# A two-layer diffusion backbone: when the first two gate slabs are split, and where the head norms are turned

## The chip, the cores and the metric

The kernel runs on one core of one Trainium2 chip, on five engines with a queue of their own each: TensorE (PE, its weight loads PEld), VectorE (DVE), ScalarE (ACT), GpSimd (POOL) and SyncE (SP), which issues the DMAs. The metric is the device time of one execution in microseconds (us), the median of a few runs.

## The reference, cut to what matters

Two layers over 512 latent and 256 context tokens, 1024 wide, in float32. The second layer needs of the context only keys and values. In each layer:

```
p = modulate(rmsnorm(x)) @ w_in           # columns: conv a | conv g | q | k | v | merge gates
z = p.a * sigmoid(p.g)                    # 512 channels
conv = silu(layernorm(depthwise31(z)))    # 31 taps along the tokens
per head of 8:
    w = softmax(q1 @ k1) - lam * softmax(q2 @ k2)
    o = rmsnorm(w @ v) * (1 - lam_init)   # a factor for each head and token
g = sigmoid(p.gates + b_gate)             # 2048 columns: g_conv | g_attn
x = x + gx1 * ((g_conv * (conv @ w_conv_out) + g_attn * (o @ w_attn_out)) @ w_out)
x = x + gx2 * (relu(modulate(rmsnorm(x)) @ w_mlp1) ** 2 @ w_mlp2)
```

## The kernel before

**Three products for one.** Each float32 matrix is split into a high part, rounded for TensorE's fast float32 format, and the low part that is left; a product is three matmuls, high by high, low by high and high by low (lines 109 to 111, and `mm3`). `split` (L75 to L77) makes them: ScalarE copies the high part (L76), VectorE subtracts (L77), or GpSimd where a call says so. A weight slab of 256 columns is loaded by one DMA (`load_slab`) and split in two halves, so two high parts of 128x1024 and two low parts. Names: `r_wg` is a raw gate slab, `h_wg` its high and `l_wg` its low part, and a slab is called (1,0) for the first of the attention half of the gates, (1,1) for the second, up to (0,3). `state["behind"]` holds instructions behind which `load_slab` queues the split on their engine (`tc.issue_after`).

**The attention stage.** Heads go one by one, `attend(h)`: scores S (L722, L724), maximum, exponentials e on ScalarE (L729), their difference on VectorE (L739), transposes wT (L752) with a split into wth and wtl, the values av (`values`, L109 to L111 with vh and vl), a square osq and a copy uo on ScalarE (L767, L769), and `finish`: two sums on TensorE (L777), rsall on ScalarE (L781) and a power on GpSimd (L784). Between these steps `merge` puts other matmuls as filler, by a ratio of costs written in the code (`rc`). With the last head, number 7, the filler is the conv branch: `conv_a`, then `conv_g` with blocks cg of 128x512 (in layer 0 also 128x256 for the context), each followed by a sigmoid sg on ScalarE (L510, which needs another activation table than the exponential: ACT_TABLE_LOAD) and the multiply z on VectorE (L512). `conv_g1_ahead` loads gate slab (1,0) behind the first block of the second half, with GpSimd as the engine of its low part, and slab (1,1) at the filler's end.

**Between attention and gates.** `spill_rstd` turns the 32 (layer 0: 48) norm factors of all heads on TensorE (rsT, L814), VectorE copies them out of PSUM (rst, L816), and SP writes them to DRAM (rs_d, L817). They come back spread over the partitions (arb, L984) and are multiplied into the head outputs ar (L986), whose low parts h1l feed the attention projection ya.

**The gates.** A loop over eight slabs, the attention half first: two gate tiles gt of 24 matmuls in each for the latent tokens, one sigmoid each (L1009). The 31 taps of the convolution for each of four channel groups (`taps`, L955 and L959, accumulator cacc) are spread over VectorE's time here, `per_gate` of them behind each gate tile. Then ya, LayerNorm and the convolution's projection yc.

**What sets the order.** The order of instructions on each engine is that in which the scheduler lets them issue: each waits its turn behind what was put on its engine before, and `issue_after` adds an edge. PSUM tiles come from pools: gt, cg and rsT share two tiles of one pool (`mm_tile`).

Of the kernel before, what the change touches and what calls it, by code (L numbers as in the profile page):

```python
# [10 lines left out]
AF = mybir.ActivationFunctionType  # L11
# [40 lines left out]
def trunk_kernel(  # L52
# [6 lines left out]
    nc = tc.nc  # L59
# [389 lines left out]
    for i in range(DEPTH):  # L449
# [50 lines left out]
        def conv_g(s):  # L500
            w = conv_w.pop(("g", s), None) or conv_load("g", s)
            for m in range(2):
                cc = 2 * s + m
                for g in groups:
# [4 lines left out]
                    sgt = ap.tile([P, 768], F32, tag="e0", name=f"sg{i}_{cc}_{g.start}", bufs=2)  # L509
                    nc.scalar.activation(out=sgt[:, :W], in_=ps[:, :W], func=AF.Sigmoid)  # L510
                    zz = zt[cc][:, z0 : z0 + W]
# [4 lines left out]

        wg = {}

        def gate_slab(half, s, lo_eng=None):
            wg[half, s] = load_slab(rows(wi, G_OFF + half * D + 256 * s, 256),  # L520
                                    f"wg{i}_{half}_{s}", lo_eng=lo_eng)

        def conv_g1_ahead():

            g = conv_g(1)
            yield next(g)
            gate_slab(1, 0, nc.gpsimd)
            yield from g
            gate_slab(1, 1)

# [162 lines left out]
        def attend(h):  # L693
# [5 lines left out]
            def scores(t):  # L699
# [15 lines left out]
                for m in range(2):  # L715
                    S = pS.tile([P, 768], F32, tag="S", name=f"S{nm}_{m}")
                    for lo, hi in ((0, 512), (512, 768)):
                        lo = max(lo, kb * P)
                        if hi <= lo:
# [8 lines left out]
                    e = ap.tile([P, 768], F32, tag=f"e{m}", name=f"e{m}{nm}", bufs=2 - m)  # L728
                    nc.scalar.activation(out=e[:, :nkey], in_=S[:, :nkey], func=AF.Exp,  # L729
                                         bias=st[:, m : m + 1],  # L730
                                         accum_out=st[:, 2 + m : 3 + m])
                    es.append(e)
# [24 lines left out]
            def values(u):  # L757
# [10 lines left out]
                uo = ap.tile([P, 256], F32, tag="uo", name=f"uo{i}_{h}_{u}")  # L768
                nc.scalar.activation(out=uo, in_=av[:, :256], func=AF.Copy, scale=L["ag"])  # L769
                nc.sync.dma_start(at_d[i][h, :, 256 * u : 256 * u + 256], uo)  # L770
# [127 lines left out]
        for h in range(H):  # L898
# [14 lines left out]
            if h == H - 1:  # L913
                rest = chain_(conv_a(0), conv_a(1), conv_g(0), conv_g1_ahead())
                rc = 24.0 if last else 38.0
            fill.append(with_late(rest))
# [4 lines left out]
            merge(main, chain_(*fill), fc / att_cost)  # L921
        drain(spill_rstd())
        for pl in (psx, pspool, apool):
# [68 lines left out]
        for half, lst in ((1, ga), (0, gc)):  # L992
            for s in range(4):
                if (half, s) not in wg:
                    gate_slab(half, s)
                if half == 0 and s == 3:
                    for hg in branch[:4]:
                        branch_load(*hg)
# [389 lines left out]
```

## Time and profile before

| | us |
|---|---|
| median of three runs | 2351.58 |
| lowest and highest | 2349.04 and 2352.13 |
| the profiled execution, its own time | 2353.61 |
| its span | 2351.8 |
| TensorE busy | 2276.6 |
| VectorE busy | 1476.0 |
| ScalarE busy | 995.2 |
| GpSimd busy | 687.3 |

The span is the time from the first to the last instruction that the profile shows; the execution's own time holds 1.8 us around it. The head that ends the attention stage of layer 0 stands at about 450 to 485 us of the span, that of layer 1 at about 1740 to 1780. A granted clock of 1.00 is TensorE's upper level of 2.4 GHz; matmuls of 128x512 that take 0.63 us where others take 0.39 ran at the lower, 1.2 GHz.

### The profile page before, as it was taken

What the parts mean: (1) busy time and instruction counts of PE and PEld (TensorE: products, weight loads), DVE (VectorE), ACT (ScalarE), POOL (GpSimd) and SP (SyncE); (2) the same over time, 40 slices, a digit from 0 to 9 for tenths busy, and PEclk for the clock granted to TensorE, in tenths of its full rate; (3) what the DMA queues carried; (4) which work ended last, traced back from release to release, by engine and by line L of the source; (5) the groups of instructions that cost most, each with busy time, mean ns of one, the idle gap of its engine ahead of it and who ended that gap; (6) DMA issues with size and microseconds to landing.
All of it is one profiled execution on the core that took longest, in us unless ns stands there. A gap on an engine that the chain in (4) does not pass through costs nothing.

```text
span 2351.8 us, 36393 instructions
## 1 busy us (share of the span) xinstructions
PE 2276.6 (97%) x14626; PEld 2042.8 (87%) x14626; DVE 1476.0 (63%) x2587; ACT 995.2 (42%) x1965; POOL 687.3 (29%) x790
## 2 busy tenths in 40 slices
PE   7999999999999999999999999999899999999999
PEld 6999998888888988888888988999877879888887
DVE  6777776699656455565655465767759966433332
ACT  5556654522332362332415255655542334432432
POOL 1866764100000133232223266757610000000000
PEclk9999999999999999999999999999999999999999
DMA  9111111143535124333343211111114323223222
GB/s 313 57 42 34 44 46 44 46 160 125 180 119 175 51 81 127 115 128 115 113 130 127 89 46 57 44 43 44 61 59 141 112 90 126 90 90 98 99 90 72
DMA packets 222570, 224.76 MB, mean 96 GB/s; under 512 B 6256, under 2 KB 212544, under 8 KB 222272
## 3 DMA queue, kind: packets, MB, share of 16 engines
q1 hardware_dynamic: 222400, 222.43, 29.4%
q8 instruction: 115, 1.88, 0.3%
q14 instruction: 55, 0.45, 0.1%
HBM read 208.73 MB, written 13.67 MB: 95 GB/s over the span
## 4 chain that ended last, share of the span: by engine, by line
PE 83%; DVE 7%; ACT 4%; POOL 2%; DMA 2%; issue 1%; SPq 0%; ACTq 0%; POOLq 0%; DVEq 0%
PE r L109 6%; PE r L110 6%; PE r L111 6%; PE f L110 6%; PE f L109 6%; PE f L111 6%; PE gt L109 3%; PE gt L110 3%; PE gt L111 3%; PE qk L109 2%; PE qk L110 2%; PE qk L111 2%; PE v L109 2%; PE v L110 2%; PE v L111 2%; PE o L109 2%
## 5 line engine op out<-in xcount | busy, mean ns | idle before, releaser
L110 PE MATMUL f<-h2l,h_w 128*128 128x512 f32 (+1 forms) x832 | 284.5, 343 | 1.1 <-POOL h2l L77 1.1
L109 PE MATMUL f<-h2h,h_w 128*128 128x512 f32 (+1 forms) x832 | 282.9, 343 | 2.2 <-ACT h2h L76 1.7
L111 PE MATMUL f<-h2h,l_w 128*128 128x512 f32 (+1 forms) x832 | 283.0, 342 | 0.0
L109 PE MATMUL r<-fh,h_w 128*128 128x512 f32 (+1 forms) x832 | 283.0, 341 | 0.0
L110 PE MATMUL r<-fl,h_w 128*128 128x512 f32 (+1 forms) x832 | 282.9, 340 | 0.0
L111 PE MATMUL r<-fh,l_w 128*128 128x512 f32 (+1 forms) x832 | 282.8, 340 | 0.0
L77 POOL TENSOR_TENSOR l_w<-r_w,h_w 128x1024 fp32r<-128x1024 f32 x64 | 157.8, 2487 | 339.5 <-ACT h_w L76 339.5
L76 ACT ACTIVATE h_w<-r_w 128x1024 fp32r<-128x1024 f32 x128 | 128.6, 1052 | 254.3 <-PE r L110 117.2
L959 DVE SCALAR_TENSOR_TENSOR cacc<-z,cols,cacc 128x783 f32<-128x783 f32 (+1 forms) x240 | 201.2, 891 | 0.3
L279 DVE SCALAR_TENSOR_TENSOR adaac<-ar,cvec,adaac 128x256 f32<-128x256 f32 x336 | 160.8, 541 | 44.6 <-DMA ar<-in_w_ada_dram 22.7
L109 PE MATMUL qk<-h_wqk,h1h 128*128 128x256 f32 x640 | 183.3, 289 | 0.7 <-ACT h1h L76 0.7
L1154 DVE SCALAR_TENSOR_TENSOR X<-r,ad,X 128x512 f32<-128x512 f32 (+1 forms) x104 | 65.1, 625 | 189.0 <-PE r L111 188.8
L110 PE MATMUL qk<-l_wqk,h1h 128*128 128x256 f32 x640 | 180.6, 284 | 0.0
L111 PE MATMUL qk<-h_wqk,h1l 128*128 128x256 f32 x640 | 176.9, 285 | 0.3 <-POOL h1l L77 0.3
L726 DVE TENSOR_REDUCE st<-S 128x1 f32<-128x768 f32 (+1 forms) x160 | 134.7, 846 | 66.8 <-PE S L724 65.3
L109 PEld LDWEIGHTS f<-h2h,h_w 128*128 128x128 f32 x832 | 158.1, 191 | 21.1 <-ACT h2h L76 2.3
L110 PEld LDWEIGHTS f<-h2l,h_w 128*128 128x128 f32 x832 | 159.1, 191 | 19.6 <-POOL h2l L77 1.9
L111 PEld LDWEIGHTS f<-h2h,l_w 128*128 128x128 f32 x832 | 158.8, 191 | 17.7
L111 PEld LDWEIGHTS r<-fh,l_w 128*128 128x128 f32 x832 | 157.7, 190 | 17.7
L109 PEld LDWEIGHTS r<-fh,h_w 128*128 128x128 f32 x832 | 157.7, 190 | 17.4
L110 PEld LDWEIGHTS r<-fl,h_w 128*128 128x128 f32 x832 | 157.8, 190 | 17.2
L1235 DVE TENSOR_TENSOR fl<-fr,fh 128x512 fp32r<-128x512 f32 (+1 forms) x104 | 67.9, 659 | 138.4 <-ACT fr L1234 138.2
(255 smaller groups left out, 6297.7 us busy)
## 6 DMA issues: line engine op xcount, KB each, us to landing
r_w<-in_w_mlp_dram SPq DMA_DIRECT2D x64, 1024.0 KB, 5.4
ada<-in_w_ada_dram SPq DMA_DIRECT2D x24, 1024.0 KB, 6.1
ar<-in_w_ada_dram SPq DMA_DIRECT2D x48, 512.0 KB, 3.5
r_wqk<-in_w_in_dram SPq DMA_DIRECT2D x32, 512.0 KB, 5.1
r_wg<-in_w_in_dram SPq DMA_DIRECT2D x16, 1024.0 KB, 5.9
r_wv<-in_w_in_dram SPq DMA_DIRECT2D x8, 1024.0 KB, 5.2
r_wao<-in_w_attn_out_dram SPq DMA_DIRECT2D x8, 1024.0 KB, 4.8
r_wo<-in_w_out_dram SPq DMA_DIRECT2D x8, 1024.0 KB, 7.3
```

The costliest lines, as they stand in the source:

```text
L76: nc.scalar.activation(out=hi, in_=src, func=AF.Copy)
L77: return (lo_eng or nc.vector).tensor_tensor(out=lo, in0=src, in1=f32(hi), op=ALU.subtract)
L109: nc.tensor.matmul(ps, sh, mh, start=first, stop=False)
L110: nc.tensor.matmul(ps, sh, ml, start=False, stop=False)
L111: nc.tensor.matmul(ps, sl, mh, start=False, stop=last)
L279: nc.vector.scalar_tensor_tensor(out=a[:, q], in0=r[:, j], scalar=cvec[:, k, q : q + 1], in1=a[:, q], op0=ALU.mult, op1=ALU.add)
L726: nc.vector.tensor_reduce(out=st[:, m : m + 1], in_=S[:, :nkey], axis=AX.X, op=ALU.max, negate=True)
L959: nc.vector.scalar_tensor_tensor(out=ca[cc][:, :CV], in0=zt[cc][:, t : t + CV], scalar=wcol, in1=ca[cc][:, :CV], op0=ALU.mult, op1=ALU.add)
L1154: state["done"] = nc.vector.scalar_tensor_tensor(out=X[:, mb, g], in0=ps[:, :W], scalar=gate[:, s, mb : mb + 1], in1=X[:, mb, g], op0=ALU. ...
L1235: state["done"] = nc.vector.tensor_tensor(out=fl[mb][:, g], in0=r[:, :W], in1=f32(fh[mb][:, g]), op=ALU.subtract).ins
```

## The change

Five edits, all in the code that both layers run:

- each conv gate's sigmoid is traced behind the exponential traced last (`exps`), and its instruction is kept (`gated`);
- gate slab (1,0) is loaded at the start of `conv_g1_ahead`, and its split queued behind the last sigmoid of the conv gate's first half;
- gate slab (1,1) is loaded behind the merge of the last head, its split queued behind that head's last copy uo (`ended`);
- `spill_rstd` moves from the end of the attention stage into the gates, ahead of slab (1,1)'s tiles;
- the filler's cost of the last head in layer 1, `rc`, is 20 in place of 24.

```diff
--- before.py
+++ after.py
@@ -507,7 +507,9 @@
                     fm_block(ps[:, :W], w, m * P, lambda k: (hh[:, k], hl[:, k]), g)
                     z0 = PAD if g is LAT else ZC
                     sgt = ap.tile([P, 768], F32, tag="e0", name=f"sg{i}_{cc}_{g.start}", bufs=2)
-                    nc.scalar.activation(out=sgt[:, :W], in_=ps[:, :W], func=AF.Sigmoid)
+                    with tc.issue_after(exps[0]):
+                        gated[:] = [nc.scalar.activation(out=sgt[:, :W], in_=ps[:, :W],
+                                                         func=AF.Sigmoid).ins]
                     zz = zt[cc][:, z0 : z0 + W]
                     nc.vector.tensor_tensor(out=zz, in0=zz, in1=sgt[:, :W], op=ALU.mult)
                     if m == 0 and g is LAT and s == 0:
@@ -515,6 +517,7 @@
                     yield 5.3 if g is LAT else 2.7
 
         wg = {}
+        exps, gated, ended = [], [], []
 
         def gate_slab(half, s, lo_eng=None):
             wg[half, s] = load_slab(rows(wi, G_OFF + half * D + 256 * s, 256),
@@ -523,10 +526,10 @@
         def conv_g1_ahead():
 
             g = conv_g(1)
-            yield next(g)
+            state["behind"] = tuple(gated)
             gate_slab(1, 0, nc.gpsimd)
+            state["behind"] = ()
             yield from g
-            gate_slab(1, 1)
 
 
         sqs = [ap.tile([P, 4, QK + 1], F32, tag=f"sqe{n}", name=f"sqe{i}_{n}", bufs=1) for n in range(2)]
@@ -726,9 +729,9 @@
                     nc.vector.tensor_reduce(out=st[:, m : m + 1], in_=S[:, :nkey], axis=AX.X,
                                             op=ALU.max, negate=True)
                     e = ap.tile([P, 768], F32, tag=f"e{m}", name=f"e{m}{nm}", bufs=2 - m)
-                    nc.scalar.activation(out=e[:, :nkey], in_=S[:, :nkey], func=AF.Exp,
-                                         bias=st[:, m : m + 1],
-                                         accum_out=st[:, 2 + m : 3 + m])
+                    exps[:] = [nc.scalar.activation(out=e[:, :nkey], in_=S[:, :nkey], func=AF.Exp,
+                                                    bias=st[:, m : m + 1],
+                                                    accum_out=st[:, 2 + m : 3 + m]).ins]
                     es.append(e)
                 nc.vector.reciprocal(st[:, 4:5], st[:, 3:4])
                 nc.vector.tensor_scalar(st[:, 5:6], st[:, 4:5], st[:, 2:3], L["nlam"],
@@ -766,7 +769,8 @@
                 sq = ap.tile([P, 256], F32, tag="osq", name=f"osq{i}_{h}_{u}", bufs=1)
                 nc.scalar.activation(out=sq, in_=av[:, :256], func=AF.Square)
                 uo = ap.tile([P, 256], F32, tag="uo", name=f"uo{i}_{h}_{u}")
-                nc.scalar.activation(out=uo, in_=av[:, :256], func=AF.Copy, scale=L["ag"])
+                ended[:] = [nc.scalar.activation(out=uo, in_=av[:, :256], func=AF.Copy,
+                                                 scale=L["ag"]).ins]
                 nc.sync.dma_start(at_d[i][h, :, 256 * u : 256 * u + 256], uo)
                 d["sq"], d["av"] = sq, av
 
@@ -912,14 +916,16 @@
                 rc = 8.1
             if h == H - 1:
                 rest = chain_(conv_a(0), conv_a(1), conv_g(0), conv_g1_ahead())
-                rc = 24.0 if last else 38.0
+                rc = 20.0 if last else 38.0
             fill.append(with_late(rest))
             fc += rc
             main = with_carry(attend(h))
             if h == H - 1:
                 main = chain_(main, rest_of(carry))
             merge(main, chain_(*fill), fc / att_cost)
-        drain(spill_rstd())
+        state["behind"] = tuple(ended)
+        gate_slab(1, 1)
+        state["behind"] = ()
         for pl in (psx, pspool, apool):
             pl.__exit__(None, None, None)
 
@@ -993,6 +999,8 @@
             for s in range(4):
                 if (half, s) not in wg:
                     gate_slab(half, s)
+                if (half, s) == (1, 1):
+                    drain(spill_rstd())
                 if half == 0 and s == 3:
                     for hg in branch[:4]:
                         branch_load(*hg)
```

No instruction's work changes. What moves on the engines is shown below; line numbers of the changed kernel are up to eight higher.

**ScalarE, end of head 7 in layer 1.** `h_wg_1_0` and `h_wg_1_1` are the high parts of the two slabs, `sg_n` the sigmoid of conv channel group n, `7_u` the query groups of head 7. Before:

```order
L76 ACTIVATE h_wg_1_0_18928<-r_wg_1_0_18926 128x1024 x2
L76 ACTIVATE wth_7_0_1_18472<-wT_7_1_1_18637 128x3x128
L729 ACTIVATE e_7_3_18766,st_7_3_18759<-S_7_3_0_18760,st_7_3_18759 128x768
L767 ACTIVATE osq_7_0_18723<-av_7_0_18704 128x256
L769 ACTIVATE uo_7_0_18725<-av_7_0_18704,ag_9370 128x256
L76 ACTIVATE wth_7_1_0_18643<-wT_7_2_0_18781 128x3x128
L781 ACTIVATE rsall_14539<-av_7_0_18704,es_7_0_18474 128x1 x2
L76 ACTIVATE wth_7_1_1_18645<-wT_7_2_1_18787 128x3x128
L510 ACT_TABLE_LOAD
L510 ACTIVATE sg_0_0_18818<-cg_0_0_18793 128x512
L510 ACTIVATE sg_1_0_18890<-cg_1_0_18865 128x512
L76 ACTIVATE wth_7_1_0_18643<-wT_7_3_0_18829 128x3x128
```

Changed:

```order
L76 ACTIVATE wth_7_0_1_18472<-wT_7_1_1_18637 128x3x128
L732 ACTIVATE e_7_3_18740,st_7_3_18733<-S_7_3_0_18734,st_7_3_18733 128x768
L770 ACTIVATE osq_7_0_18689<-av_7_0_18670 128x256
L772 ACTIVATE uo_7_0_18691<-av_7_0_18670,ag_9370 128x256
L76 ACTIVATE wth_7_1_0_18643<-wT_7_2_0_18781 128x3x128
L785 ACTIVATE rsall_14539<-av_7_0_18670,es_7_0_18474 128x1 x2
L76 ACTIVATE wth_7_1_1_18645<-wT_7_2_1_18787 128x3x128
L511 ACT_TABLE_LOAD
L511 ACTIVATE sg_0_0_18854<-cg_0_0_18829 128x512
L511 ACTIVATE sg_1_0_18895<-cg_1_0_18870 128x512
L76 ACTIVATE h_wg_1_0_18900<-r_wg_1_0_18898 128x1024 x2
L76 ACTIVATE wth_7_1_0_18643<-wT_7_3_0_18793 128x3x128
```

Slab (1,0) goes from ahead of wT's high part to behind the second sigmoid; slab (1,1) from ahead of the last sigmoid to behind the last copy, further on than the rows shown.

**TensorE, end of the attention stage in layer 1.** Before, from the last values to the first gate tile:

```order
L109 MATMUL av_7_1_18841<-wth_7_1_1_18645,vh_3_17349 128x256
L110 MATMUL av_7_1_18841<-wtl_7_1_1_18646,vh_3_17349 128x256
L111 MATMUL av_7_1_18841<-wth_7_1_1_18645,vl_3_17350 128x256
L777 MATMUL av_7_1_18841<-cst,osq_7_1_18860 128x1 x2
L814 MATMUL rsT_18970<-cst,rsall_14539 32x128
L109 MATMUL gt_1_0_0_18989<-h1h_9379,h_wg_1_0_18928 128x512
```

Changed, the end of the second gate tile and the start of the third:

```order
L111 MATMUL gt_1_1_0_19017<-h1h_9379,l_wg_1_0_18901 128x512
L109 MATMUL gt_1_1_0_19017<-h1h_9379,h_wg_1_0_18900 128x512
L110 MATMUL gt_1_1_0_19017<-h1l_9380,h_wg_1_0_18900 128x512
L781 MATMUL av_7_1_18805<-cst,osq_7_1_18824 128x1 x2
L111 MATMUL gt_1_1_0_19017<-h1h_9379,l_wg_1_0_18901 128x512
L818 MATMUL rsT_19049<-cst,rsall_14539 32x128
L109 MATMUL gt_1_2_0_19055<-h1h_9379,h_wg_1_1_18964 128x512
L110 MATMUL gt_1_2_0_19055<-h1l_9380,h_wg_1_1_18964 128x512
```

The sums (L777, now L781) and rsT stand behind 47 gate matmuls, with one more between them.

**VectorE in layer 1, around the split of slab (1,1).** The rows of cacc are taps. Before:

```order
L959 SCALAR_TENSOR_TENSOR cacc_18987<-z_18497,cols_9344,cacc_18987 128x512 x3
L77 TENSOR_TENSOR l_wg_1_1_18965<-r_wg_1_1_18962,h_wg_1_1_18964 128x1024
L959 SCALAR_TENSOR_TENSOR cacc_18987<-z_18497,cols_9344,cacc_18987 128x512
L77 TENSOR_TENSOR l_wg_1_1_18965<-r_wg_1_1_18962,h_wg_1_1_18964 128x1024
L959 SCALAR_TENSOR_TENSOR cacc_18987<-z_18497,cols_9344,cacc_18987 128x512
L512 TENSOR_TENSOR z_18497<-z_18497,sg_3_0_18959 128x512
L959 SCALAR_TENSOR_TENSOR cacc_18987<-z_18497,cols_9344,cacc_18987 128x512 x2
L816 COPY rst_18972<-rsT_18970 32x128
```

Changed:

```order
L965 SCALAR_TENSOR_TENSOR cacc_18982<-z_18497,cols_9344,cacc_18982 128x512 x2
L514 TENSOR_TENSOR z_18497<-z_18497,sg_3_0_18959 128x512
L965 SCALAR_TENSOR_TENSOR cacc_18982<-z_18497,cols_9344,cacc_18982 128x512 x3
L961 TENSOR_SCALAR cacc_18982<-z_18497,cols_9344 128x512
L965 SCALAR_TENSOR_TENSOR cacc_18982<-z_18497,cols_9344,cacc_18982 128x512 x7
L77 TENSOR_TENSOR l_wg_1_1_18965<-r_wg_1_1_18962,h_wg_1_1_18964 128x1024
L965 SCALAR_TENSOR_TENSOR cacc_18982<-z_18497,cols_9344,cacc_18982 128x512 x2
L77 TENSOR_TENSOR l_wg_1_1_18965<-r_wg_1_1_18962,h_wg_1_1_18964 128x1024
L965 SCALAR_TENSOR_TENSOR cacc_18982<-z_18497,cols_9344,cacc_18982 128x512 x5
L820 COPY rst_19051<-rsT_19049 32x128
```

The last conv gate's multiply z is ahead of the slab, the slab behind the taps that follow it, and the copy of the norm factors behind the slab and seven taps.

**VectorE in layer 0, around the split of head 7's last weights.** `sg_1_512` is the sigmoid over the context. Before:

```order
L512 TENSOR_TENSOR z_5402<-z_5402,sg_1_0_5960 128x512
L77 TENSOR_TENSOR wtl_7_2_0_5778<-wT_7_4_0_5963,wth_7_2_0_5777 128x2x128
L959 SCALAR_TENSOR_TENSOR cacc_6163<-z_5402,cols_113,cacc_6163 128x783 x3
L512 TENSOR_TENSOR z_5402<-z_5402,sg_1_512_6010 128x256
L959 SCALAR_TENSOR_TENSOR cacc_6163<-z_5402,cols_113,cacc_6163 128x783
L955 TENSOR_SCALAR cacc_6163<-z_5402,cols_113 128x783
L959 SCALAR_TENSOR_TENSOR cacc_6163<-z_5402,cols_113,cacc_6163 128x783
L77 TENSOR_TENSOR wtl_7_2_0_5778<-wT_7_5_0_5968,wth_7_2_0_5777 128x2x128
```

Changed:

```order
L514 TENSOR_TENSOR z_5402<-z_5402,sg_1_0_5960 128x512
L77 TENSOR_TENSOR wtl_7_2_0_5778<-wT_7_4_0_5963,wth_7_2_0_5777 128x2x128
L965 SCALAR_TENSOR_TENSOR cacc_6158<-z_5402,cols_113,cacc_6158 128x783
L514 TENSOR_TENSOR z_5402<-z_5402,sg_1_512_6010 128x256
L965 SCALAR_TENSOR_TENSOR cacc_6158<-z_5402,cols_113,cacc_6158 128x783
L961 TENSOR_SCALAR cacc_6158<-z_5402,cols_113 128x783
L965 SCALAR_TENSOR_TENSOR cacc_6158<-z_5402,cols_113,cacc_6158 128x783 x3
L77 TENSOR_TENSOR wtl_7_2_0_5778<-wT_7_5_0_5968,wth_7_2_0_5777 128x2x128
```

The context's multiply goes ahead of two taps; what stands in front of the last wtl is the same in sum.

## Rows read from the trace of the kernel before

**Rows 1.** The page: span, and busy time of each engine.
```profile
span 2351.8 us, 36393 instructions
...
PE 2276.6 (97%) x14626; PEld 2042.8 (87%) x14626; DVE 1476.0 (63%) x2587; ACT 995.2 (42%) x1965; POOL 687.3 (29%) x790
```

**Rows 2.** Windows: length, busy us of PE, PEld, DVE, ACT, POOL, clock, DMA.
```profile
450.00:460.00 10.00, 6.76 (x44) 5.49 (x43) 5.03 (x11) 6.28 (x13) 1.14 (x3) 1.00 0.02 7
1750.00:1760.00 10.00, 5.32 (x25) 4.13 (x25) 7.05 (x9) 5.11 (x11) 4.96 (x5) 0.82 0.37 120
1800.00:1820.00 20.00, 20.00 (x90) 16.55 (x89) 20.00 (x29) 6.33 (x8) 0.00 (x0) 1.00 0.40 128
```

**Rows 3.** Timeline, layer 1's first place: start, us, instruction, [idle before <-releaser].
```profile
1747.33 2.01 ACT L76 ACTIVATE h_wg<-r_wg 128x1024 fp32r<-128x1024 f32 x2 [1.96 <-PE cg L110]
...
1747.47 0.49 PE L752 MATMUL wT<-cst,e 128*128 128x128 f32 x3
...
1748.47 4.69 POOL L77 TENSOR_TENSOR l_wg<-r_wg,h_wg 128x1024 fp32r<-128x1024 f32 x2 [9.48 <-ACT h_wg L76]
...
1749.24 0.47 ACT L76 ACTIVATE wth<-wT 128x384 fp32r<-128x384 f32 x1
...
1750.94 3.03 DVE L739 SCALAR_TENSOR_TENSOR e<-e,st,e 128x768 f32<-128x768 f32 x1
...
1753.89 0.54 DVE L77 TENSOR_TENSOR wtl<-wT,wth 128x384 fp32r<-128x384 f32 x1
...
1757.53 0.79 PE L109 MATMUL cg<-h1h,h_wcg 128*128 128x512 f32 x1 [2.49 <-ACT sg L510]
```

**Rows 4.** Groups by line on VectorE, 1650 to 1747 and 1757.5 to 1878.
```profile
L739 DVE SCALAR_TENSOR_TENSOR e<-e,st,e 128x768 f32<-128x768 f32 x9 | 9.8, 1085 | 0.2
...
L959 DVE SCALAR_TENSOR_TENSOR cacc<-z,cols,cacc 128x512 f32<-128x512 f32 x120 | 82.2, 742 | 0.0
```

**Rows 5.** Timeline, layer 1's second place, TensorE and VectorE.
```profile
1776.19 0.61 PE L777 MATMUL av<-cst,osq 128*128 128x1 f32 x4 [1.69 <-ACT uo L769]
...
1778.76 0.39 PE L814 MATMUL rsT<-cst,rsall 128*32 128x128 f32 x1 [1.96 <-POOL rsall L784]
...
1779.38 0.63 PE L110 MATMUL gt<-h1l,h_wg 128*128 128x512 f32 x1
...
1780.65 0.27 DVE L816 COPY rst<-rsT 32x128 f32<-32x128 f32 x1
...
1783.94 0.39 PE L109 MATMUL gt<-h1h,h_wg 128*128 128x512 f32 x1
...
1792.68 0.69 DVE L986 TENSOR_TENSOR ar<-ar,arb 128x512 f32<-128x512 f32 x1
```

**Rows 6.** What VectorE waited for, 1758 to 1878: us, times, longest.
```profile
DVE l_wg L77 <- ACT h_wg L76: 1.7, 3, 0.6
...
DVE l_wao L77 <- ACT h_wao L76: 1.2, 1, 1.2
```

**Rows 7.** Timeline, layer 1's attention projection, VectorE and TensorE.
```profile
1873.71 0.69 DVE L77 TENSOR_TENSOR h1l<-ar,h1h 128x512 fp32r<-128x512 f32 x1
...
1874.45 0.50 PE L110 MATMUL ya<-h1l,h_wao 128*128 128x512 f32 x1
```

**Rows 8.** Timeline, the same place in layer 0, VectorE, GpSimd and TensorE.
```profile
467.39 5.19 DVE L959 SCALAR_TENSOR_TENSOR cacc<-z,cols,cacc 128x783 f32<-128x783 f32 x3
...
469.09 5.75 POOL L77 TENSOR_TENSOR l_wg<-r_wg,h_wg 128x1024 fp32r<-128x1024 f32 x2
...
472.50 2.62 DVE L512 TENSOR_TENSOR z<-z,sg 128x256 f32<-128x256 f32 x1
...
478.00 0.39 PE L110 MATMUL av<-wtl,vh 128*128 128x256 f32 x1 [1.24 <-DVE wtl L77]
...
480.36 2.92 DVE L959 SCALAR_TENSOR_TENSOR cacc<-z,cols,cacc 128x783 f32<-128x783 f32 x3
...
483.19 0.41 DVE L512 TENSOR_TENSOR z<-z,sg 128x256 f32<-128x256 f32 x1
```

## The prediction

> **What bounds the kernel now.** Read the page first: the span is 2351.8 us and TensorE is busy for 2276.6 of it [rows 1], so only a place where it stands still, or runs at the lower clock, can give time back. The change touches two such places, once per layer: the end of the last attention head and the start of the gates. The windows come second [rows 2]. In layer 1 the ten microseconds from 1750 hold 5.32 of TensorE work at a mean granted clock of 0.82; in layer 0 the same place, from 450, holds 6.76 at 1.00. From 1800 on TensorE has no gap at all, but neither has VectorE: 20.00 of 20.
>
> The chain at the first place in layer 1 [rows 3]: the transposes wT of 1747.47 are over at 1747.96, but ScalarE has taken the two halves of a gate slab (2.01 us from 1747.33) and comes to wT's high part at 1749.24. VectorE's multiply of the exponentials then takes 3.03 us, beside GpSimd's two low parts of the same slab, which run from 1748.47 for 4.69 in all; nine others of that multiply took 1.085 [rows 4]. The split wtl is at 1753.89, and TensorE starts its next convolution block at 1757.53 after 2.49 of idleness.
>
> The second place [rows 5]: TensorE waits 1.69 us for ScalarE's copy of the last head, does the two sums (L777), waits 1.96 for GpSimd's power, turns the norm factors (rsT) and starts the gates at the lower clock: gt takes 0.63 where it takes 0.39 later. From the second of them at 1779.38 to the thirteenth at 1783.94 pass 4.56 us; eleven steps of the spacing in [rows 2], 90 in 20.00 us or about 0.22 each, would be 2.4, so a fall of the clock costs 2.1 us, 2.2 with the slower first one.
>
> **The change part by part, layer 1.** *Slab (1,0) behind the sigmoid.* The order puts its two ScalarE halves behind the first sigmoids, and its GpSimd halves there too. By [rows 3] the high part of wT is 1749.24 - 1748.00 = 1.24 earlier, and the multiply costs 1.02 to 1.09 instead of 3.03. Followed through (values 1.05 earlier, ScalarE's square and copy and the next high part the same, wtl then no longer behind the long multiply), wtl comes at about 1751.7 instead of 1753.89, and the block at 1755.3 instead of 1757.5: **-2.2 us**. The idle time left there is about 3.3 us in 4.3; a spell of 3.24 in ten left the clock at 1.00 in layer 0, and 1.69 + 1.96 within 4.3 us was followed by half clock in layer 1 [rows 2, 5]. Whether the clock falls is open, worth 2.2.
>
> *Slab (1,1) behind the last copy, norm factors in the gates.* The 1.69 goes, because 48 gate matmuls now stand between the last values and what waits for the copy. The 1.96 stays almost whole: the new order leaves one gate matmul (0.23) between the two sums and rsT. But TensorE is then through two gate tiles and about 5.9 us ahead of before if the clock holds after that wait, 3.5 if not.
>
> That lead runs into VectorE. The first cost is GpSimd's halves, now beside the taps of the convolution. Layer 0 shows that price in the kernel before [rows 8]: while GpSimd split its slab (5.75 us from 469.09), three taps took 5.19 against 2.92 later and a gate multiply 2.62 against 0.41, together 4.5 us. Layer 1's pair took 4.69 [rows 3] and cost the one multiply beside it 2.0. Bounds: 0 to 5.75; I take 4.2, nearest to layer 0, because there too one tap follows another. The Trainium skill, "GPSIMD Engine Reference", section "8. Key points", says that GpSimd shares its SBUF interfaces with VectorE and that they contend when VectorE reads two SBUF inputs; taps do. By that rule the stall must come; without it the gain would be the first rival's. For that reason I give that rival no more than a quarter.
>
> VectorE's sum up to the last split h1l, on which the attention projection ya waits: start 2.2 earlier; stall +4.2; the waits of before, 1.7 + 1.2 [rows 6], absorbed, -2.9; two taps of 0.67 (82.2 us for 120 [rows 4], overlapped) moved behind the last h1l, -1.3: in all **-2.2**. Against it: the rsT copy on VectorE stands behind slab (1,1) and five taps, at about 1791.5, and before 12.0 us passed from that copy (1780.65) to the first product with a factor (1792.68) [rows 5]. VectorE reaches that product at about 1802.5, so it may wait 1 us there (0 to 2; the DMA of the factors moves with the copy, behind two loads of the heads on SP). I take +0.5. Before, ya's matmul at 1874.45 began just as its split of 1873.71 ended (1874.40) [rows 7]: TensorE has no slack against VectorE there, so what it gains beyond VectorE's 1.7 it waits off. New waits for slab (1,1)'s low parts and for the factor copy (a fourth gate tile needs the PSUM that rsT holds, about 0.6) lie inside that lead and cost nothing. LayerNorm's sums now stand behind more of ya, up to four matmuls or 0.9 us later: +0.4. Layer 1: **-1.3**, from -6 (no stall) to +1.
>
> **Layer 0.** The first sigmoid does not move. On VectorE the same items stand in front of the low part of the last turned weights (wtl), in another order (the context's gate multiply is earlier), so it comes when it did, or up to 0.65 later since GpSimd starts behind one more sigmoid. On TensorE four gate matmuls of 128x256, 0.12 apart, no longer fill the time before, so it arrives 0.4 to 0.5 earlier at the wait that was 1.24 [rows 8]. It is lost: behind it TensorE and VectorE have no gap, and nothing gives it back. Bounds +0.4 to +1.6, I take **+1.0**. The norm factors come later here too, behind twelve taps, with the next use far off: 0. The lower ratio of fill (24 to 20, layer 1 only) is in the order that I followed, no term of its own.
>
> **The sum**: -1.3 + 1.0 = -0.3 on the profiled run of 2353.61 us, 2353.3. That run was 2.0 above the median 2351.58 of the three runs shown, so the forecast for a median is **2351.3 us**: no difference that could be told from none, since about 0.2%, 4.7 us, is what a measurement of this kernel can tell.
>
> **Rivals.** *A, the stall is small.* If GpSimd's halves meet VectorE as they met one multiply, or are hidden by its own waits, VectorE is 6 us earlier at ya, TensorE's lead of 5.9 lasts, and and a clock that holds at the first place may add up to 2.2 where VectorE allows it: -5.9 + 0.4, with +0.4 in layer 0, -5.1: about 2346.5. For it: 2.0 is all that layer 1 showed [rows 3, 4]; against it layer 0 [rows 8]. It decides when the stall is under 1 us.
>
> *B, the wait comes back as a fall of the clock (slower).* TensorE, 5.9 ahead, stands at ya for VectorE in one piece of 3.5 us, as long as the 3.65 after which the clock fell [rows 5], and pays 2.2 behind it; layer 0's wait grows to between 1.7 and 2.9 and pays as much. With the upper end of that wait: -1.3 + 2.2 + 1.6 + 2.2 = +4.7, about 2356.3. It decides if the clock falls behind the wait at ya as it fell behind those 3.65; in layer 0 alone it would not be seen. Against it: layer 0 kept 1.00 through 3.24 [rows 2].
>
> *C, nothing moves.* VectorE's chain, with stall and late factors, ends when it ended; layer 0 loses nothing: 2351.6.
>
> **How the numbers follow.** Forecast 0.45, A 0.27, B 0.17, C 0.11. Faster by over 0.2%: A and a tail of the forecast, less the part of A that stays within, 0.27. Slower: B with tails, 0.18. Within: 0.55. The range takes the bounds of the stall, of the clock and of layer 0's wait: 2346.0 to 2356.3.
>
> **What would show it.** Right: the multiply beside wT at about 1.1 in layer 1 and the convolution block some 2 us earlier; taps stretched by about 4 us beside GpSimd's l_wg from about 1757; the wait for the copy (L769) gone, the one for rsall at 1.7; TensorE waiting on h1l at ya; in layer 0 a wait on wtl of 1.6 to 2.9. Wrong: no stretched taps, or no wait at ya with the lead kept to the end (A); rows of 0.63 behind ya or behind layer 0's wait (B). The forecast falls if the first sigmoid in either layer moves, which the order denies, or if the factors' loads hold VectorE for more than 2 us.

## The result: slower by 0.18%

The changed kernel took 2357.06 us in the median of 17 runs (2351.62 to 2362.56), the kernel before 2351.84 in 17 (2349.04 to 2358.37). The measured ratio is 1.0018, with a 95% interval of 1.0009 to 1.0026: 4.2 us, between 2.1 and 6.1 (the two medians alone are 5.2 apart). The forecast was 2351.3 with a range up to 2356.3, so the time lies outside it, on the side of rival B. The profiled execution took 2359.20 us.

The page of the changed kernel, to be read against [rows 1]:

```profile
span 2357.4 us, 36391 instructions
...
PE 2282.2 (97%) x14626; PEld 2047.1 (87%) x14626; DVE 1479.8 (63%) x2587; ACT 995.2 (42%) x1965; POOL 684.9 (29%) x790
```

TensorE is busy for 5.6 us more, though no matmul was added, and the span is 5.6 longer: in sum it is not idle for longer. What grew is the time of matmuls at half clock, and waits changed places. But one pair of executions doesn't tell this change's part. The matmuls of the two traces, set side by side, part by 1.2 us in the first 20 us of the program, by 1.5 at 829 and by 1.5 at 1705, at places that the change doesn't touch: there the clock fell in one execution and not in the other. So the time is followed from one mark to the next, inside the stage that was changed.

The marks of layer 1: the start of the last score matmul (S), the end of the last split h1l, the start of the last matmul of ya, and the starts of the first and of the last matmul of yc. Times in us from the first mark, worked from the traces (of before: S at 1743.01, so h1l ends 135.06 later):

| kernel | h1l ends | last ya | first yc | last yc | against before |
|---|---|---|---|---|---|
| before | 135.06 | 171.77 | 173.10 | 199.34 | |
| changed | 135.36 | 172.77 | 175.46 | 202.37 | +3.0 |

Layer 1 loses 3.0 us, which is most of the 4.2. What TensorE waited for there, in the changed kernel, from 1740 to 1930 (us in total, times, longest):

```profile
PE cg L109 <- ACT sg L511: 2.5, 1, 2.5
PE gt L109 <- ACT g L1017: 2.4, 1, 2.4
PE yc L118 <- ACT ch L1074: 2.3, 1, 2.3
PE ya L110 <- DVE h1l L77: 2.1, 2, 1.3
PE rsT L818 <- POOL rsall L788: 1.6, 1, 1.6
PE ya L109 <- DVE g L1095: 0.6, 1, 0.6
PE yc L118 <- DVE g L1131: 0.6, 1, 0.6
PE av L781 <- ACT uo L772: 0.5, 1, 0.5
PE wT L755 <- DVE wtl L77: 0.4, 1, 0.4
```

The rows of the same view and window in the kernel before that [rows 3] and [rows 5] don't show:

```profile
PE wT L752 <- DVE wtl L77: 1.5, 1, 1.5
PE yc L118 <- ACT ch L1066: 1.3, 2, 0.9
...
PE av L109 <- ACT wth L76: 0.8, 1, 0.8
```

Gone are the 1.69 for the copy (0.5 is left, of the head's other half), the wait for wth and most of those for wtl. New are 2.4 for a sigmoid g ahead of a gate tile, 2.1 for h1l, and 2.3 for ch where it was 1.3.

### The profile page after: what moved, and what is told of

Read it like the earlier page. It is cut to its first block, busy times and chain, and to the rows that moved or that the text cites. A ratio compares the mean times of both kernels' runs of the same rounds, so it can differ in the third digit from the quotient of the medians.

```text
span 2357.4 us, 36391 instructions
## 1 busy us (share of the span) xinstructions
PE 2282.2 (97%) x14626; PEld 2047.1 (87%) x14626; DVE 1479.8 (63%) x2587; ACT 995.2 (42%) x1965; POOL 684.9 (29%) x790
## 4 chain that ended last, share of the span: by engine, by line
PE 82%; DVE 9%; ACT 3%; POOL 3%; DMA 2%; issue 1%; SPq 0%; ACTq 0%; DVEq 0%; POOLq 0%
PE r L109 6%; PE r L111 6%; PE r L110 6%; PE f L110 6%; PE f L109 6%; PE f L111 6%; PE gt L109 3%; PE gt L110 3%; PE gt L111 3%; PE qk L109 2%; PE qk L110 2%; PE qk L111 2%; PE v L109 2%; PE yc L118 2%; PE o L109 2%; PE o L111 2%
```

## Where layer 1's gain went

The first place came out as forecast, and so did the price that VectorE paid for it. Timeline of the changed kernel, VectorE, GpSimd and TensorE, to be read against [rows 3]:

```profile
1753.01 1.02 DVE L742 SCALAR_TENSOR_TENSOR e<-e,st,e 128x768 f32<-128x768 f32 x1
...
1758.50 0.79 PE L109 MATMUL cg<-h1h,h_wcg 128*128 128x512 f32 x1 [2.49 <-ACT sg L511]
...
1760.82 5.34 POOL L77 TENSOR_TENSOR l_wg<-r_wg,h_wg 128x1024 fp32r<-128x1024 f32 x2 [4.41 <-ACT h_wg L76]
...
1761.06 2.87 DVE L965 SCALAR_TENSOR_TENSOR cacc<-z,cols,cacc 128x512 f32<-128x512 f32 x1
...
1763.85 2.60 DVE L961 TENSOR_SCALAR cacc<-z,cols 128x512 f32<-128x512 f32 x1
```

The multiply of the exponentials takes 1.02 where it took 3.03, and the block of the conv gate starts 2.3 us earlier, counted from the last score. GpSimd's halves now meet the taps: a tap takes 2.87 for 0.75, the first tap of the next group 2.60 for 0.54, so 2.1 each. The TENSOR_SCALAR among the two has one tensor in SBUF, and is held up as long.

Then the third gate tile. Timeline, TensorE, ScalarE and VectorE:

```profile
1788.47 0.34 PE L818 MATMUL rsT<-cst,rsall 128*32 128x128 f32 x1 [1.64 <-POOL rsall L788]
...
1789.11 1.21 DVE L77 TENSOR_TENSOR l_wg<-r_wg,h_wg 128x1024 fp32r<-128x1024 f32 x1
...
1790.43 0.69 ACT L1017 ACTIVATE g<-gt,cols 128x512 f32<-128x512 f32 x1 [2.86 <-DVE l_wg L77]
...
1791.17 0.80 PE L109 MATMUL gt<-h1h,h_wg 128*128 128x512 f32 x1 [2.36 <-ACT g L1017]
...
1791.76 0.63 PE L110 MATMUL gt<-h1l,h_wg 128*128 128x512 f32 x1
```

After rsT TensorE stands for 2.36 us: its PSUM tile comes free with the sigmoid g of the second gate tile, and that sigmoid waited 2.86 for VectorE's second low part of slab (1,1), 1789.11 to 1790.32. The sigmoid doesn't read the slab. In the changed kernel it waits for semaphores of TensorE, VectorE and GpSimd, in the kernel before for TensorE's alone (worked from the traces). The kernel text offers a reason, which no run tests: the tile that the sigmoid writes comes from a pool that takes over memory of the attention stage's pool, where the raw slab lay. The gate matmuls behind the wait are at half clock (0.63), eight of them. The kernel before had such a fall behind its rsT too, so the lower clock is not gone but later, and the one at the conv gate is there as before.

So TensorE's lead is spent before it reaches ya, and with it goes the saving on VectorE. What VectorE waited for between the first sigmoid and the last h1l:

```profile
DVE ar L992 <- DMA arb<-rs_d: 1.0, 2, 0.7
...
DVE h1l L77 <- ACT h1h L76: 0.9, 1, 0.9
...
DVE l_wg L77 <- ACT h_wg L76: 0.8, 2, 0.6
...
DVE l_wao L77 <- ACT h_wao L76: 0.6, 1, 0.6
```

In the kernel before, besides [rows 6]:

```profile
DVE h1l L77 <- ACT h1h L76: 0.2, 1, 0.2
```

These waits add up to 3.17 us before and 3.27 in the changed kernel (worked from the traces). The 1.04 for the loads of the norm factors (arb) is new; the waits for ScalarE's high parts fell only from 3.17 to 2.23. ScalarE's high parts wait until TensorE is done with the slab before (28.9 us in seven waits on gate matmuls from 1800 to 1882); when TensorE is late, they are late too. The other executions fit: in e4, e6 and e9 (below), where TensorE keeps its lead, VectorE waits for no slab's high part, and in e7, where TensorE stood 4.2 us for rsT, for 3.5 us.

The tail, timeline of VectorE and TensorE from the last h1l on:

```profile
1880.95 0.69 DVE L77 TENSOR_TENSOR h1l<-ar,h1h 128x512 fp32r<-128x512 f32 x1
...
1881.56 1.54 DVE L965 SCALAR_TENSOR_TENSOR cacc<-z,cols,cacc 128x512 f32<-128x512 f32 x2
...
1883.01 1.28 DVE L1095 TENSOR_TENSOR g<-g,ya 128x512 f32<-128x512 f32 x2
...
1883.75 0.50 PE L109 MATMUL ya<-h1h,h_wao 128*128 128x512 f32 x1 [0.59 <-DVE g L1095]
...
1894.77 1.02 PE L1039 MATMUL ln<-tot,cst 128*128 128x512 f32 x2
...
1921.75 0.80 PE L118 MATMUL yc<-ch,h_wco 128*128 128x512 f32 x1 [2.30 <-ACT ch L1074]
...
1922.34 0.63 PE L118 MATMUL yc<-ch,l_wco 128*128 128x512 f32 x1
```

Two taps moved behind the last h1l, and the multiply g that frees a PSUM tile for ya's third block is behind them: TensorE waits 0.59. The first LayerNorm sum (ln) now comes behind two more whole tiles of ya, at 1894.77, 148.5 us behind the last score instead of 136.6. So yc waits 2.30 for ch, 1.36 us more than before between the last ya and the first yc, and starts at half clock.

## The experiments

Theory S says that GpSimd's slab (1,0), beside the taps in layer 1, is the cause: VectorE falls 4.2 us behind, and what waits for VectorE (slab (1,1)'s low parts, h1l) takes the gain. Its rivals: layer 0 loses the time (T2); slab (1,1) and the norm factors lose it; LayerNorm's place (L); chance (T3). The stage's column below is the start of the last yc behind the last score, against before's 199.34, and doesn't hold what chance does elsewhere; the ratio does.

| kernel | h1l ends | first yc | last yc | stage | ratio to before, 95% |
|---|---|---|---|---|---|
| e1, layer 1 only | 135.47 | 175.58 | 202.55 | +3.2 | 1.0023, 1.0008 to 1.0037 |
| e2, layer 0 only | 135.58 | 173.62 | 199.86 | +0.5 | 0.9997, 0.9986 to 1.0008 |
| e3, slab (1,0) only | 138.49 | 179.03 | 205.91 | +6.6 | 1.0031, 1.0021 to 1.0041 |
| e4, slab (1,1) and norms | 131.57 | 169.58 | 195.81 | -3.5 | 0.9993, 0.9980 to 1.0005 |
| e5, low (1,0) on VectorE | 128.66 | 169.23 | 195.48 | -3.9 | 0.9981, 0.9968 to 0.9994 |
| e6, (1,0) back in layer 1 | 131.88 | 170.79 | 197.03 | -2.3 | 0.9986, 0.9972 to 1.0000 |
| e7, (1,0) behind the exponential | 134.65 | 172.22 | 198.47 | -0.9 | 0.9981, 0.9969 to 0.9994 |
| e8, slab (1,1) only | 133.81 | 172.46 | 198.70 | -0.6 | 0.9998, 0.9986 to 1.0011 |
| e9, e7 with low parts on VectorE | 130.62 | 168.63 | 194.87 | -4.5 | 0.9997, 0.9982 to 1.0012 |
| e10, e5 again | 128.65 | 169.25 | 196.12 | -3.2 | 0.9990, 0.9975 to 1.0004 |
| e11, low (1,1) on GpSimd too | 136.52 | 174.54 | 200.77 | +1.4 | 1.0019, 1.0006 to 1.0033 |
| e12, e5 in layer 1 only | 128.65 | 169.22 | 195.46 | -3.9 | 1.0002, 0.9989 to 1.0016 |

### One layer at a time

e1 makes each edit conditional on the second layer, e2 on the first (with the old ratio 24):

```diff
-            state["behind"] = tuple(gated)
-            gate_slab(1, 0, nc.gpsimd)
-            state["behind"] = ()
-            yield from g
+            if last:                     # e2: if not last
+                state["behind"] = tuple(gated)
+                gate_slab(1, 0, nc.gpsimd)
+                state["behind"] = ()
+                yield from g
+            else:
+                yield next(g)
+                gate_slab(1, 0, nc.gpsimd)
+                yield from g
+                gate_slab(1, 1)
...
-                if (half, s) == (1, 1):
+                if last and (half, s) == (1, 1):
```

> The change in layer 1 alone, layer 0 in the old order. Theory T1 (layer 1 gives its gain back: the first place wins 2.3 us, then a wait of about 2.4 us of the third gate tile's start for a sigmoid that itself waits for slab (1,1)'s low parts, lower clock behind it, then waits on h1l and LayerNorm): +2 to +4 us against before, as the whole change. T2 (layer 0 is where the time is lost): within 1 us of before. T3 (the trace's difference is made of falls of the clock elsewhere, which come by chance): within 1 us of before as well, and the new wait of 2.4 us shows all the same.

> The change in layer 0 alone, layer 1 in the old order. T1: -1 to +0.5 us against before; in the trace a wait of 1.5 on the last wtl, lower clock for some gate matmuls, and the lost time given back at the attention projection ya, whose wait on h1h of 2.2 us gets shorter. T2: +3 to +5 us. T3: within 1 us.

e1 carries the whole loss, 1.0023 (+5.4 us, above the +2 to +4 expected), and its stage is the changed kernel's to 0.2 us. In this execution fewer matmuls of the conv gate ran at half clock (7 for 14), and rsT waited 3.1 us for 1.6; the third gate tile starts 44.9 us behind the last score all the same, since both times it waits for VectorE. e2 is within 0.2%: T2 falls. T3 falls as the account of the result, since the loss is there again in another execution, in the stage and in the time. What TensorE waited for in e2's layer 0:

```profile
PE av L110 <- DVE wtl L77: 1.5, 1, 1.5
...
PE ya L109 <- ACT h1h L76: 2.1, 1, 2.1
```

The wait for wtl is 1.5 where it was 1.24 [rows 8], and the last gate matmul comes 0.3 later, counted from the last score. The wait at ya did not get shorter by more than 0.1, against the expectation; the last ya is 1.2 earlier all the same, because the half clock that followed the wait at ya in the kernel before is not in this execution.

### One slab at a time

e3 has slab (1,0) alone, e4 slab (1,1) and the norm factors alone, e8 slab (1,1) alone (against the changed kernel):

```diff
 e3
+            gate_slab(1, 1)              # at the end of the fill, as before
-                rc = 20.0 if last else 38.0
+                rc = 24.0 if last else 38.0
-        state["behind"] = tuple(ended)
-        gate_slab(1, 1)
-        state["behind"] = ()
+        drain(spill_rstd())
-                if (half, s) == (1, 1):
-                    drain(spill_rstd())
 e4, and e8 with spill_rstd back as well
-            state["behind"] = tuple(gated)
+            yield next(g)
             gate_slab(1, 0, nc.gpsimd)
-            state["behind"] = ()
             yield from g
```

> Only the first slab (1,0) behind the conv gate's sigmoid, in both layers; slab (1,1), the norm factors and the fill ratio as before. T1: the first place of layer 1 keeps its gain of 2.3 us, the multiply takes 1.0 us, GpSimd's halves stretch two VectorE instructions by 2.1 us each; the wait for the copy of the last head (1.7) and for the power (2.0) are as before, nothing waits for slab (1,1). VectorE's delay of 4.2 - 2.3 = 1.9 us shows at ya: within 1.5 us of before. T2: as the whole change if layer 0's loss is in this slab, +3 or more.

> Slab (1,0) as before, slab (1,1) behind the last copy and the norm factors in the gates as changed. T1: the first place of layer 1 has its 2.5 + 1.5 + 0.8 us of waits again; the sums' wait of 1.7 is gone, the wait of the third gate tile of about 2.4 us is there or longer, with the lower clock behind it: +1 to +4 us against before. If the loss is GpSimd's stall on VectorE instead, this one is faster than before by 1 to 3 us.

> Only slab (1,1) behind the last copy, with the lower fill ratio; slab (1,0) and the norm factors as before. If the norm factors' move carries the 3.5 us that the pair gained in layer 1: the waits for the copy (1.7) and for the power (2.0) stand between attention and gates as before, time within 1 us of before. If slab (1,1) carries it: -2 to -4 us.

e3 is slower than before by 0.31%, and its stage loses 6.6 us, more than the whole change's 3.0; in the time the two are not clearly apart (their intervals share 1.0021 to 1.0026). Expected was within 1.5 us of before. TensorE's waits there show why, from 1740 to 1800:

```profile
PE av L110 <- DVE wtl L77: 3.3, 1, 3.3
...
PE rsT L819 <- POOL rsall L789: 2.6, 1, 2.6
```

VectorE comes late to the last weights of the attention (wtl, 3.3 where no wait was), and GpSimd's power later still. In the whole change gate matmuls hide that wait, and the price shows behind them.

e4 is the other half: its stage gains 3.5 us. Its waits from 1740 to 1930:

```profile
PE ya L110 <- DVE h1l L77: 1.7, 1, 1.7
...
PE rsT L817 <- POOL rsall L787: 1.0, 1, 1.0
...
PE yc L118 <- ACT ch L1073: 1.3, 2, 0.9
```

No gate tile waits for a sigmoid, rsT waits 1.0, and ch 1.3 as before. Expected was a wait of 2.4 at the third gate tile and +1 to +4; that was for the theory that slab (1,1) is the cause, and it is not there. For GpSimd's stall as the cause -1 to -3 was expected; 0.9993 is -1.6, with an interval that holds 0. With slab (1,0) where it was, VectorE is 4 us less behind and slab (1,1)'s low parts are in time. e8 keeps 0.6 of the 3.5, so most of the gain needs the norm factors moved as well; in the time neither e4 nor e8 can be told from before. These are single executions.

### The low parts of slab (1,0) on VectorE

e5 and e10 are the same kernel; e12 does it in layer 1 alone, with `None if last else nc.gpsimd`:

```diff
-            gate_slab(1, 0, nc.gpsimd)
+            gate_slab(1, 0)
```

> The whole change, but slab (1,0)'s low parts on VectorE in place of GpSimd. Theory S (slab (1,0)'s loss in layer 1 is GpSimd's stall of VectorE, 4.2 us, against 2.3 for the two subtractions on VectorE): no instruction of 2.6 to 2.9 us near 1760, the last h1l about 1.9 us earlier than in the changed kernel, and 1 to 3 us faster than it, so +1 to +3 us against before. Theory L (the loss is LayerNorm's sums, which the order puts behind two more tiles of ya whenever slab (1,0) is split late): ya ends earlier but the wait of yc on ch stays at 2 us or grows, and the time is that of the changed kernel, +4 to +6.

> The whole change with slab (1,0)'s low parts on VectorE in both layers, a second time. Theory S: -3 to -6 us against before as the first time; if the first time was chance, within 2 us of before.

> The whole change with slab (1,0)'s low parts on VectorE in layer 1 alone, on GpSimd in layer 0. Theory S: layer 1 carries the gain, so -3 to -6 us against before, as with both layers. Rival (layer 0's stall of 4.3 us was the larger part): 0 to +3.

This takes GpSimd's work away and gives VectorE 2.3 us of it. Timeline of VectorE in e5, and below it what it waited for up to the last h1l:

```profile
1766.08 1.22 DVE L77 TENSOR_TENSOR l_wg<-r_wg,h_wg 128x1024 fp32r<-128x1024 f32 x1
...
1767.21 0.55 DVE L961 TENSOR_SCALAR cacc<-z,cols 128x512 f32<-128x512 f32 x1
...
1767.67 1.22 DVE L77 TENSOR_TENSOR l_wg<-r_wg,h_wg 128x1024 fp32r<-128x1024 f32 x1
```

```profile
DVE ar L992 <- DMA arb<-rs_d: 0.8, 2, 0.5
...
DVE h1l L77 <- ACT h1h L76: 0.5, 1, 0.5
```

No tap is stretched. The last h1l ends at 128.66, 6.7 us earlier than in the changed kernel, where the direct saving is only 4.2 - 2.3 = 1.9. The rest is the chain: slab (1,1)'s low parts are in time, no gate tile waits for a sigmoid, no gate matmul runs at half clock, and VectorE's waits for the slabs' high parts are gone (the 0.8 and 0.6 for l_wg and l_wao are not in the list). Fewer matmuls of the conv gate are at half clock too, 7 for 14, but that is not the cause: e1 has the same 7 and the whole loss. LayerNorm's order is the late one here, and yc waits 2.3 as in the changed kernel: L's cost is real, 1.3 us between ya and yc, but it is not what makes the loss. The three executions agree in the stage to 0.7 us. The time, measured against before, is below the changed kernel's both times (the intervals 0.9968 to 0.9994 and 0.9975 to 1.0004 end below 1.0009).

The sizes were not foreseen. Both theories put e5 above before's time, S by 1 to 3 us and L by 4 to 6; it came out 4.5 below. e10, at -2.4, is between "faster again" and "chance", and its interval holds 0. e12's 1.0002 is less than the -3.9 us of its stage would give, and it is what its rival, layer 0's stall, expected. Against that rival stand e2, which has that stall alone and loses nothing, and layer 0's own last yc, 1.0 later than before's in e5 and 0.3 earlier in e10, which is no gain. So in the time the effect of the low parts on VectorE is shown for both layers together, and for layer 1 alone only in the stage.

### Slab (1,0) where VectorE has time

e6 keeps slab (1,0) where it was in layer 1. e7 queues it behind both of the last exponentials there, e9 is e7 with the low parts on VectorE:

```diff
 e7, e9
-                    exps[:] = [nc.scalar.activation(out=e[:, :nkey], ...
+                    exps[:] = exps[-1:] + [nc.scalar.activation(out=e[:, :nkey], ...
-            state["behind"] = tuple(gated)
+            state["behind"] = tuple(exps if last else gated)
 e9
-            gate_slab(1, 0, nc.gpsimd)
+            gate_slab(1, 0, None if last else nc.gpsimd)
 e6
+            if last:
+                yield next(g)
+                gate_slab(1, 0, nc.gpsimd)
+            else:
                 state["behind"] = tuple(gated)
                 gate_slab(1, 0, nc.gpsimd)
                 state["behind"] = ()
```

> The whole change in layer 0; in layer 1 all but slab (1,0), which is split where it was before. Both theories: layer 1 as in the run without slab (1,0), the last ya 3.5 us earlier than before, and layer 0 about 1 us earlier: -2 to -5 us against before.

> The whole change, but in layer 1 slab (1,0)'s split stands behind the last exponential and the high part of the turned weights, ahead of the last square and copy, so that GpSimd works while VectorE has little to do and ahead of the taps. ScalarE's square comes up to 1 us later than in the changed kernel. Theory S: no stretched tap, the convolution block starts 1 to 2 us earlier than before, -3 to -6 us against before. Theory L: LayerNorm's sums are back behind the first two tiles of ya, so the same. If a tap is stretched all the same, -1 to -3.

> The whole change, but in layer 1 slab (1,0)'s split stands behind the last exponential and its low parts are on VectorE, ahead of the taps, where VectorE waits for ScalarE anyway. Theory S (GpSimd's work beside VectorE's is what costs): the two subtractions of 1.2 us fall into VectorE's idle time before the first sigmoid, the first place keeps 1 to 2 us of gain, the last h1l is at or below the 128.7 us behind the last score that low parts on VectorE behind the sigmoid gave: -4 to -7 us against before. Rival (ScalarE's two halves delay the square and the copy, so the first place's gain is gone): -1 to -3.

e6 has e4's stage but for one fall of the clock behind a wait of 2.1 at ya (eight matmuls at 0.63), as rival B described it: -2.3 for -3.5. Its time is 3.3 us under before's, in the range expected, but the interval reaches 1.0000 and layer 0 was not earlier: its last yc came 4.3 us later. e7 stretches no tap, and its stage gains only 0.9, less than expected; GpSimd's rows show where it goes:

```profile
1746.74 4.84 POOL L77 TENSOR_TENSOR l_wg<-r_wg,h_wg 128x1024 fp32r<-128x1024 f32 x2 [0.46 <-PE av L111]
...
1780.59 3.89 POOL L788 TENSOR_TENSOR rsall<-rsall,mhalf 128x2 f32<-128x2 f32 x1 [28.33 <-ACT rsall L785]
```

The slab is done at 1751.58, ahead of the taps. But the power of the norm factors, at 1780.59, takes 3.89 us, and TensorE waits 4.2 for it. Beside VectorE's work the same power took 1.34 in the changed kernel, 2.80 in e1, whose layer 1 is the same program, and 0.80 to 1.98 in the others; so this may be chance of the one execution. e7's time, 0.9981, is better than a stage of -0.9 would give. e9's two subtractions come right behind the multiply, ahead of the first sigmoid:

```profile
1746.37 1.02 DVE L742 SCALAR_TENSOR_TENSOR e<-e,st,e 128x768 f32<-128x768 f32 x1
...
1747.31 2.35 DVE L77 TENSOR_TENSOR l_wg<-r_wg,h_wg 128x1024 fp32r<-128x1024 f32 x2
```

Its stage is the shortest, -4.5, and the first place keeps 1.0 of the 2.3, against the rival. But the last h1l is at 130.62, not at or below the 128.7 that theory S expected, and the time, 0.9997, shows none of the 4 to 7 us, though the interval reaches to -4.

### A second dose

e11 puts slab (1,1)'s low parts on GpSimd too, in layer 1:

```diff
-        gate_slab(1, 1)
+        gate_slab(1, 1, nc.gpsimd if last else None)
```

> The whole change, and in layer 1 slab (1,1)'s low parts on GpSimd too: a second dose of the same. Theory S: two more VectorE instructions stretched by 2.1 us each against 2.3 saved, so the last h1l 1.5 to 2 us later than in the changed kernel unless the third gate tile's wait goes; GpSimd's power for the norm factors comes behind the slab, so the wait of rsT grows by 2 us or more: +4 to +9 us against before. Rival (only the wait of slab (1,1)'s low parts behind taps costs): these now come earlier, the wait of 2.4 us goes, and the time falls to before's or under it.

Timeline of GpSimd and VectorE at the second slab, and two of TensorE's waits:

```profile
1775.90 5.06 POOL L77 TENSOR_TENSOR l_wg<-r_wg,h_wg 128x1024 fp32r<-128x1024 f32 x2 [15.17 <-ACT h_wg L76]
...
1776.12 2.62 DVE L961 TENSOR_SCALAR cacc<-z,cols 128x512 f32<-128x512 f32 x1
```

```profile
PE gt L109 <- DVE rst L820: 3.8, 1, 3.8
...
PE rsT L818 <- POOL rsall L788: 2.1, 1, 2.1
```

Again two VectorE instructions are stretched (2.62 and one of 2.85), and the last h1l is 1.2 later than in the changed kernel. The third gate tile now waits for nothing, as the rival said. But VectorE begins the copy of the norm factors (rst) only 9.2 us behind the start of rsT, where it was 5.1, and the fourth gate tile waits 3.8 for the PSUM tile that the copy frees. So the wait moved and grew, the time did not fall, and the rival's price does not hold. The wait for the power grew by 0.5, not by the 2 expected. The stage is +1.4, under the changed kernel's +3.0, since LayerNorm is back in its early place; the time, 1.0019, is the changed kernel's, at the lower end of what was expected.

## Why the prediction was wrong

- **The first place, -2.2 us**: right, -2.3. The clock did fall there again, as in the kernel before.
- **The stall, +4.2**: right in size, 2.13 + 2.06, and in place. That it meets a TENSOR_SCALAR as well as a tap fits what the Trainium skill says in "GPSIMD Engine Reference", "8. Key points", which names a 2-port mode beside two SBUF inputs; the trace shows the 2.60 and not the mode.
- **The waits of before absorbed, -2.9**: the step that failed first. The waits for high parts fell by 0.9, from 3.17 to 2.23. I took them for slack of VectorE's own; they are set by TensorE's pace, and are absorbed only while TensorE keeps its lead. In e5, where it does, 0.5 is left.
- **The loads of the factors, +0.5**: 1.04, inside the bounds of 0 to 2.
- **New waits "lie inside that lead and cost nothing"**: the second. The third gate tile waited 2.36, not 0.6, for a sigmoid that I had not followed, and the clock fell behind it. I had set TensorE's lead at 5.9 and let that cover the new waits; 2.1 of it was left at ya's first matmul, and none behind ya's two waits for h1l. Together: h1l +0.3 against the -1.7 of the sum.
- **Two taps behind the last h1l, -1.3**: they were saved ahead of h1l and paid behind it, by g and ya's third block (+0.7 from the last h1l to the last ya). The tap itself is 82.2/120 = 0.685, not 0.67, which changes nothing.
- **LayerNorm, +0.4**: mis-sized. Its first sum moved behind 48 more matmuls of ya, not four; the stretch from the last ya to the first yc is 1.36 us longer, and the half clock behind it costs 0.7 more: +2.0.
- **The sum for layer 1**: 0.3 + 0.7 + 1.4 + 0.7 = +3.0, where I had -1.3.
- **Layer 0, +1.0**: +0.3 in the last gate matmul, under the lower bound of 0.4, and -1.0 at the layer's last yc. "Nothing gives it back" did not hold: TensorE waits at ya for ScalarE's h1h, 2.2 us in the kernel before, and there the clock falls behind that wait, which costs 1.4. The traces divide by the place of slab (1,0) in layer 0: the clock falls in all four with the old place (before, e1, e4, e8), and in one (e6) of the eight with it moved and GpSimd at work. That looks like more than chance; its cause is open.
- **The rivals**: B was right in its direction and in that falls of the clock come back, but its place was another: at the third gate tile and at yc, not at ya. In e6 it did come at ya. A got a chance of 0.27 though the text allows it no more than a quarter; with a stall of 4.2 it is out.

What stays open is how much of the stage's gain a better version brings to the whole. The three executions with low parts on VectorE behind the sigmoid (e5, e10, e12) gain 3.2 to 3.9 us in the stage, and stand at 0.9981, 0.9990 and 1.0002 in the time. The two intervals that end below 1, e5's and e7's, come from one chip, on which e5 to e8 ran; none of e9 to e12, on another, is clear of before on the fast side. Outside the stage the profiled executions differ by up to 11 us (span less stage, from 2148 in e7 to 2159 in e5). Layer 0's stage, marked in the same way, lasts from 296.3 (e7) to 303.0 (e6) with the same code in that layer. So a dozen runs are too few to tell. Nor is the changed kernel's whole loss placed: layer 1's stage has +3.0 of it, and e1 loses 5.4 in the time with +3.2 there.

## What to carry to other kernels

Moving GpSimd's work off one late VectorE instruction is worth little if it lands beside VectorE's busiest stretch: price it by both places, and look for a stretch where VectorE waits for something else. An idle spell of an engine that is waiting for a paced neighbour is not slack to be absorbed; ask whose lead it depends on. And when work moves, follow what waits for the memory and the PSUM tile that it holds, not just who reads its result.

## What the runs showed of the hardware

- GpSimd holds up VectorE: two halves of 128x1024 on GpSimd (5.34 us) stretched two VectorE instructions by 2.1 us each, one with two tensors in SBUF and one with a single tensor, and so again in e1, e3 and e11. The same two halves took 2.35 us on VectorE in e9, less than the 4.2 it lost beside GpSimd.
- GpSimd's power on 128x2 took 0.73 us while VectorE was idle, and from 0.80 (e8) to 3.89 (e7) beside VectorE's work. What sets it within that range is not shown.
- The same 36 thousand instructions spread over 2349 to 2358 us in the kernel before, and the mean granted clock goes with the time: over all its executions here, 0.991 to 0.992 in the three fastest (2346.5 to 2347.0 us) and 0.987 to 0.988 in the three slowest (2359.5 to 2360.2). Matmuls at half speed are found in one execution and not in the other at 829 and 1705 us here, each spell worth about 1.5 us.
